# A streaming layer on one core: early weights and stores on GpSimd's queue, and a head's rows fetched by halves

## The chip, the cores and the metric

The kernel runs on one core of a Trainium2 chip. Its time is the device time of one execution in microseconds (us); the figure that counts is the median of several timed runs. Five engines work side by side, each through its own instruction queue in order: PE (matmuls), DVE and ACT (element-wise work), POOL (GpSimd), and SP, which here only issues DMA transfers. GpSimd and ACT can issue transfers too.

## The reference

One inference step of a hybrid layer for 1024 new positions of one stream and 64 of another that has 512 cached keys. All is float32; T = 1088 positions, 1024 channels.

```python
xn = _rmsnorm(x, p['norm_mix_w'])
proj = xn @ p['w_in']
z, xbc, dt_raw, q, k, v, gate_ssm, gate_att = jnp.split(proj, np.cumsum(IN_SIZES)[:-1].tolist(), axis=-1)
xbc_c, conv_new = _causal_dwconv(conv_past, xbc, p['ssm_conv_w'], p['ssm_conv_b'])
...
y_ssm = y_ssm * jax.nn.silu(z)
...
q = _partial_rope(_rmsnorm(q.reshape(b, t, 2 * ATT_HEADS, ATT_HEAD_DIM), p['q_norm_w']), q_pos)
k = _partial_rope(_rmsnorm(k.reshape(b, t, 2 * ATT_HEADS, ATT_HEAD_DIM), p['k_norm_w']), q_pos)
...
o = _diff_attention(q, k_all, v_all, q_pos, k_pos, lam)
o = (_rmsnorm(o, p['subln_w']) * (1.0 - lambda_init)).reshape(b, t, ATT_V_WIDTH)
mix = jax.nn.sigmoid(gate_ssm) * (y_ssm @ p['w_branch_ssm']) + jax.nn.sigmoid(gate_att) * (o @ p['w_branch_attn'])
x = x + mix @ p['w_out']
...
x = x + (jax.nn.silu(hc) * hb) @ p['w_down']
```

In the attention each of 8 heads has two score matrices (two halves, `c` = 0 and 1). Each is softmaxed by itself, and the weights are p0 - lam * p1:

```python
s = jnp.einsum('bqhd,bkhd->bhqk', q, k, preferred_element_type=jnp.float32) * (ATT_HEAD_DIM ** -0.5)
visible = (k_pos[None, :] // CHUNK) <= (q_pos[:, None] // CHUNK)
s = jnp.where(visible[None, None], s, -jnp.inf)
p = jax.nn.softmax(s, axis=-1).reshape(b, ATT_HEADS, 2, nq, -1)
a = p[:, :, 0] - lam * p[:, :, 1]
return jnp.einsum('bhqk,bkhe->bqhe', a.astype(v.dtype), v)
```

## The kernel before

Every float32 operand of a large product is split into a high and a low part, and a product is three matmuls (L156 to L158: high x high, low x high, high x low). The stages follow each other: norm of x with the first values, q, values, k, then attention, the scan of the state-space part, the two branches, the feed-forward part. An instruction scheduler turns the program into one fixed order for each engine; it works from the program's order, priorities (`tc.high_priority`) and pins (`tc.issue_after(x)`: not ahead of x on its queue). What waits for what at run time is then a matter of semaphores: an instruction that waits holds up all that stands behind it on its engine.

The stage of the keys (`heads(B_K, ...)`) ends by writing each of 8 blocks of keys three times: as output (`out_dram<-qr`, L509) and as high and low part into the scratch tensor `k_st` (L480; ACT makes `qh`, DVE makes `ql`, two buffers each). A head reads 64 channels out of all 8 blocks, so its rows can be loaded only when all 16 stores into `k_st` have landed. The queries lie in `q_st` in the same form, the cached keys in `c_st`.

For a head, `head_tiles(h)` loads by SP's queue: `q_t`, `kh_t` and `kl_t` (queries, high and low keys) for both halves, values `v_t`, and the cached `ch_t`, `cl_t`, `cv_t`. A full tile of q, kh or kl is 544 KB, in one or two transfers. `q_t`, `kh_t` and `kl_t` have 3 buffers each, so beside a head's two halves one half of the next fits. `attend(h, i, ...)` works on one block of 128 queries: scores `sc` of both halves (L707, L708), maximum, exponential, difference, then transposes `pt` (L736) and the product with the values `po` (L755). `ATT_ORDER` has the blocks in the order 7, 0, 6, 1, 5, 2, 8, 4, 3.

Attention alone leaves PE with gaps. A generator `stream()` fills them: it yields units of projection (one unit is 24 matmuls into one bank `mm`, over 384 or 320 positions), first gate tiles 15 and 14, then z tiles 0 to 3, then convolution tiles and so on (`ORDER`). `fill(1.9)` after each block takes on average 1.9 units. Each tile (three units) needs one weight block: `raw_weights` loads it (`w_f`, L142), ACT makes `w_hi` (L149), DVE `w_lo` (L150). A gate unit is evacuated by ACT into `gt` and stored into `g_sc` (L594); a z unit by ACT into `zr` (L602) and DVE (L603), and stored into `z_sc` (L604). `gt` and `zr` share three staging buffers. The scheduler lays the first 18 units (six of gates, twelve of z) ahead of head 0's first score.

All of these loads and stores go through `load`, which is SP's queue.

Of the kernel before, what the change touches and what calls it, by code (L numbers as in the profile page):

```python
# [17 lines left out]
P = 128  # L18
D = 1024
KT = D // P  # L20
TP, TS = 1024, 64
# [33 lines left out]
LAST = 200  # L55
ATT_STEPS = 1.9
SCAN_STEPS = 1.5
BRANCH_AT = 4
# [17 lines left out]
def hybrid_layer(ctx: ExitStack, tc: tile.TileContext, xT, xN, prm, cst, rope, wvd, win, wbs, wba, wout, wup, wdn,  # L76
# [53 lines left out]
    extra, turn, ahead, quick, asked, decayed, lowered = None, 0, AHEAD_IN, QUICK, None, None, None  # L130
    emptied = None, None

    def raw_weights(block, k, m, pool=None):
        nonlocal turn
        if pool is None:
            turn = (turn + 1) % 3
        p, b = (pool, 1) if pool is not None else (extra, 1) if extra is not None and turn == 0 else (wp, 2)
        w = p.tile([P, WMAX], F32, name="w_f", tag="w_f", bufs=b)
        hi = p.tile([P, WMAX], R32, name="w_hi", tag="w_hi", bufs=b)
        lo = p.tile([P, WMAX], R32, name="w_lo", tag="w_lo", bufs=b)  # L140
        w, hi, lo = (t[:, : k * m].rearrange("p (k m) -> p k m", k=k) for t in (w, hi, lo))
        load(out=w, in_=block.rearrange("p (k m) -> p k m", k=k))  # L142
        return w, hi, lo
# [8 lines left out]

    def product(ps, terms):
        n = len(terms)
        for i, (a_hi, a_lo, b_hi, b_lo) in enumerate(terms):
            PE.matmul(ps, a_hi, b_hi, start=i == 0, stop=False)  # L156
            PE.matmul(ps, a_hi, b_lo, start=False, stop=False)  # L157
            PE.matmul(ps, a_lo, b_hi, start=False, stop=i == n - 1)  # L158

# [428 lines left out]
    def gate_tiles(tiles):  # L588
        for j in tiles:
            def evac(ps, c, w):  # L590
                nonlocal last_gate
                gt = staged("gt")[:, :w]
                last_gate = act(gt, ps, AF.Tanh, scale=0.5)
                load(out=g_sc[P * j : P * (j + 1), c : c + w], in_=gt)  # L594

            yield from project(win[B_G + j], evac)

    def z_tiles(tiles):
        for j in tiles:
            def evac(ps, c, w):  # L600
                zr = staged("zr")[:, :w]
                act(zr, ps, AF.Tanh, scale=0.5)  # L602
                V.scalar_tensor_tensor(zr, zr, 1.0, ps, ALU.add, ALU.mult)  # L603
                load(out=z_sc[P * j : P * (j + 1), c : c + w], in_=zr)  # L604

# [35 lines left out]
    def stream():  # L641
        for kind, which in ORDER:
            yield from {"c": conv_tiles, "z": z_tiles, "g": gate_tiles}[kind](which)
# [15 lines left out]
    with (tc.tile_pool(name="ak", bufs=1) as ak, tc.tile_pool(name="at", bufs=1) as at,  # L659
          tc.tile_pool(name="psc", bufs=1, space=PSUM) as psc, tc.tile_pool(name="psa", bufs=1, space=PSUM) as pa):  # L660
        def head_tiles(h):
            def fetch(name, n, b, parts):
                t = ak.tile([P, n], R32, name=name, tag=name, bufs=b)
# [12 lines left out]
            ch_t = [fetch("ch_t", PAST, 2, [(0, ck[c][0:64]), (64, ck[c][0:64])]) for c in range(2)]  # L676
            cl_t = [fetch("cl_t", PAST, 2, [(0, ck[c][64:128]), (64, ck[c][64:128])]) for c in range(2)]
            cv_t = ak.tile([P, 4, P], F32, name="cv_t", tag="cv_t", bufs=1)
            load(out=cv_t, in_=cv[:, P * h : P * (h + 1)].rearrange("(a p) e -> p a e", p=P))
            return q_t, kh_t, kl_t, ch_t, cl_t, v_t, cv_t  # L680

        def attend(h, i, tiles, o_t, ssq, s0):
# [7 lines left out]
            for c in range(2):  # L690
# [6 lines left out]
                sc.append(ps)  # L697
                for a in range(0, nk, 512):
                    b = min(512, nk - a)
                    if i < 8:  # L700
                        r_hi, r_lo = kh_t[c][:, a : a + b], kl_t[c][:, a : a + b]
                    elif a == 0:
                        r_hi, r_lo = ch_t[c], cl_t[c]
                    else:
                        r_hi, r_lo = kh_t[c][:, TP:T], kl_t[c][:, TP:T]
                    lhs = q_t[c][:, P * i : P * i + n]
                    PE.matmul(ps[:n, a : a + b], lhs, r_hi, start=True, stop=False)  # L707
                    PE.matmul(ps[:n, a : a + b], lhs, r_lo, start=False, stop=True)  # L708
                if both is None:
# [74 lines left out]

        tiles = head_tiles(0)
        lam = at.tile([P, 4], F32, name="lam")
# [808 lines left out]
```

## Time and profile before

| | |
|---|---|
| three timed runs | 2453.03, 2453.19, 2457.49 us; median 2453.19 |
| the profiled execution | 2448.89 us, span 2447.1 us, mean granted clock 0.999 |
| PE, weight loads, DVE, ACT, POOL busy | 99%, 96%, 65%, 47%, 27% |
| SP's DMA queue (q1) | 385.06 MB, 49.6% of 16 engines |
| GpSimd's DMA queue (q0) | 8.91 MB, 2.4% |
| key stores into `k_st` issued | 337.6 to 378.9 us |
| attention and what fills it | from about 400 to about 1110 us |

The span runs from the first to the last instruction; the execution's own time is 1.8 us longer. Times in the views are us from the span's start. The view of waits lists who waited for whom, with total, count and longest wait; the timeline has start, duration, engine, source line, output and inputs, and in brackets the idle time before. A matmul's duration overlaps its neighbours, so matmuls are best compared from start to start. `SPq` is SP's queue: start of an issue and how long it took; when the data has landed is another matter.

### The profile page before, as it was taken

The numbers are of one execution on the slowest core, as the hardware profiler recorded it, in microseconds if no ns is written. First come the engines' busy times: TensorE is split into PE (matmuls) and PEld (weight loads), VectorE is DVE, ScalarE is ACT, GpSimd is POOL, SyncE is SP. The second block draws the span as 40 slices with busy tenths as digits, with TensorE's granted clock in tenths as the row PEclk, the third lists the DMA queues.
The fourth block names the chain that finished last, engine by engine and source line by source line (L and its number), as shares of the span: only waits on it lengthen the run. The fifth ranks groups of instructions, "written<-read, shape, count | busy, mean of one in ns | idle before, by whom it ended". The sixth has DMA issues, their size and how long they took to land. (4 is left out here: it accounts for less than half of the span.)

```text
span 2447.1 us, 44586 instructions
## 1 busy us (share of the span) xinstructions
PE 2423.5 (99%) x16956; PEld 2350.1 (96%) x16956; DVE 1602.0 (65%) x2755; ACT 1139.8 (47%) x2497; POOL 664.8 (27%) x696
## 2 busy tenths in 40 slices
PE   9999999999999999999999999999999999999998
PEld 8999999999999999999899989999999999999998
DVE  7426254865777667646767785656777777787766
ACT  6334243644565555437664653224543334353532
POOL 0000000100011001004333333103367666755434
PEclk9999999999999999999999999999999999999999
DMA  4218158554453453345679765656234343467874
GB/s 172 84 57 288 64 207 265 142 158 126 131 162 110 130 169 104 98 157 186 217 255 323 223 199 186 193 176 189 63 125 140 117 153 116 147 202 207 218 181 159
DMA packets 269319, 403.55 MB, mean 165 GB/s; under 512 B 33296, under 2 KB 202000, under 8 KB 268976
## 3 DMA queue, kind: packets, MB, share of 16 engines
q1 hardware_dynamic: 258432, 385.06, 49.6%
q0 software_dynamic: 4608, 8.91, 2.4%
q10 hardware_dynamic: 6064, 6.72, 0.8%
q8 instruction: 133, 2.18, 0.4%
q14 instruction: 82, 0.67, 0.1%
HBM read 267.04 MB, written 133.56 MB: 164 GB/s over the span
## 5 line engine op out<-in xcount | busy, mean ns | idle before, releaser
L156 PE MATMUL mm<-xn_hi,w_hi 128*128 128x384 f32 (+1 forms) x1416 | 469.9, 332 | 0.9 <-DVE zr L603 0.9
L158 PE MATMUL mm<-xn_hi,w_lo 128*128 128x384 f32 (+1 forms) x1416 | 468.6, 331 | 0.5 <-DVE w_lo L150 0.5
L157 PE MATMUL mm<-xn_lo,w_hi 128*128 128x384 f32 (+1 forms) x1416 | 467.7, 330 | 0.0
L156 PEld LDWEIGHTS mm<-xn_hi,w_hi 128*128 128x128 f32 x1416 | 266.7, 188 | 4.8 <-issue 1.6
L158 PEld LDWEIGHTS mm<-xn_hi,w_lo 128*128 128x128 f32 x1416 | 266.5, 188 | 3.4 <-issue 1.5
L157 PEld LDWEIGHTS mm<-xn_lo,w_hi 128*128 128x128 f32 x1416 | 266.7, 188 | 2.3 <-issue 1.1
L150 DVE TENSOR_TENSOR w_lo<-w_f,w_hi 128x1024 fp32r<-128x1024 f32 x116 | 147.1, 1270 | 117.9 <-ACT w_hi L149 117.5
L1254 PE MATMUL mx<-n,wh 128*128 128x272 f32 x1076 | 206.0, 289 | 0.7 <-ACT u L1398 0.4
L1254 PE MATMUL mx<-m,w_hi 128*128 128x272 f32 x1010 | 192.9, 289 | 4.2 <-DVE down L1412 4.2
L149 ACT CAST w_hi<-w_f 128x1024 fp32r<-128x1024 f32 x116 | 121.4, 1048 | 145.2 <-PE mm L157 87.5
L1254 PEld LDWEIGHTS mx<-n,wh 128*128 128x128 f32 x1076 | 169.2, 189 | 1.1 <-ACT u L1398 0.6
L1254 PEld LDWEIGHTS mx<-m,w_hi 128*128 128x128 f32 x1010 | 159.3, 189 | 4.6 <-issue 2.8
L1254 PE MATMUL mx<-n,wl 128*128 128x272 f32 x538 | 155.6, 289 | 0.0
L156 PE MATMUL mm<-b_hi,w_hi 128*128 128x384 f32 (+1 forms) x448 | 145.8, 327 | 0.6 <-DVE b_g L224 0.6
L1254 PE MATMUL mx<-m,w_lo 128*128 128x272 f32 x505 | 145.9, 289 | 0.0
L158 PE MATMUL mm<-b_hi,w_lo 128*128 128x384 f32 (+1 forms) x448 | 144.8, 324 | 0.6 <-DVE w_lo L150 0.6
L157 PE MATMUL mm<-b_lo,w_hi 128*128 128x384 f32 (+1 forms) x448 | 145.1, 325 | 0.0
L721 ACT ACTIVATE p_t<-sc,mx 128x1024 f32<-128x1024 f32 (+5 forms) x144 | 106.2, 739 | 76.4 <-DVE mx L712 37.5
L632 DVE SCALAR_TENSOR_TENSOR cc<-pre,par,cc 128x384 f32<-128x384 f32 (+1 forms) x216 | 126.6, 586 | 20.1 <-ACT cc L630 14.9
L620 POOL COPY pre<-pre 128x3 f32<-128x3 f32 x48 | 13.6, 282 | 454.5 <-ACT pre L621 343.6
L1039 ACT CAST w_hi<-ws 128x512 fp32r<-128x512 f32 (+1 forms) x62 | 37.6, 607 | 150.0 <-PE mx L1254 99.2
L618 POOL MEMSET pre<- 128x3 f32 x24 | 2.4, 101 | 383.9 <-PE mx L158 308.5
(418 smaller groups left out, 6735.7 us busy)
## 6 DMA issues: line engine op xcount, KB each, us to landing
w_f<-in_win_dram SPq DMA_DIRECT2D x76, 512.0 KB, 4.1
w_f<-in_wup_dram SPq DMA_DIRECT2D x44, 512.0 KB, 3.8
hr<-q_sc SPq DMA_DIRECT2D x70, 272.0 KB, 4.8
bc<-a_sc SPq DMA_DIRECT2D x32, 512.0 KB, 5.9
q_sc<-hb SPq DMA_DIRECT2D x44, 272.0 KB, 2.3
gb<-q_sc SPq DMA_DIRECT2D x44, 272.0 KB, 3.8
x_sc<-cc SPq DMA_DIRECT2D x48, 192.0 KB, 2.5
q_sc<-gb SPq DMA_DIRECT2D x33, 272.0 KB, 2.3
```

Of the source, the lines that this page charges most:

```text
L149: S.copy(hi, w)
L150: lowered = V.tensor_tensor(out=lo, in0=w, in1=hi, op=ALU.subtract)
L156: PE.matmul(ps, a_hi, b_hi, start=i == 0, stop=False)
L157: PE.matmul(ps, a_hi, b_lo, start=False, stop=False)
L158: PE.matmul(ps, a_lo, b_hi, start=False, stop=i == n - 1)
L618: G.memset(pre[:, 0:3], 0.0)
L620: G.tensor_copy(pre[:, 0:3], tail)
L632: V.scalar_tensor_tensor(cc[:, :m], pre[:, i : i + m], cw(i), cc[:, :m], ALU.mult, ALU.add)
L721: act(p_t[:n, :nk], sc[c][:n, :nk], AF.Exp, bias=mx[:n, c : c + 1], accum_out=dst)
L1039: S.copy(hi, src)
L1254: PE.matmul(ps, w[x][:, c], b[y][:, k], start=start and k == t == 0, stop=k == nk - 1 and t == 2, skip_group_check=not start)
```

## The change

Three things are changed.

1. Nine weight loads (`early_w` counts down from 10) and the stores of the first two entries of `ORDER` (gates 15 and 14, z 0 to 3: 18 stores) are issued by GpSimd instead of SP.
2. `head_tiles` is a generator in three steps: q, kh, kl of half 0; then of half 1 with the values; then the cached rows. Head 0's first two steps are asked for with a high priority. For the later heads the first step is asked for in the head before, at the sixth block (`ASK = 5`), the others at the head's start.
3. In a head's first block (7), a filling unit is taken between the two halves' scores, and half 1's scores are pinned behind its last matmul. That unit comes off the budget of `fill`.

```diff
+ASK = 5
...
     def raw_weights(block, k, m, pool=None):
-        nonlocal turn
+        nonlocal turn, early_w
+        early_w -= 1
...
-        load(out=w, in_=block.rearrange("p (k m) -> p k m", k=k))
+        (G.dma_start if early_w > 0 else load)(out=w, in_=block.rearrange("p (k m) -> p k m", k=k))
...
     def product(ps, terms):
+        nonlocal produced
...
-            PE.matmul(ps, a_lo, b_hi, start=False, stop=i == n - 1)
+            produced = PE.matmul(ps, a_lo, b_hi, start=False, stop=i == n - 1)
...
-                load(out=g_sc[P * j : P * (j + 1), c : c + w], in_=gt)
+                (G.dma_start if early else load)(out=g_sc[P * j : P * (j + 1), c : c + w], in_=gt)
...
-                load(out=z_sc[P * j : P * (j + 1), c : c + w], in_=zr)
+                (G.dma_start if early else load)(out=z_sc[P * j : P * (j + 1), c : c + w], in_=zr)
...
     def stream():
-        for kind, which in ORDER:
+        nonlocal early, early_w
+        early_w = 10
+        for n, (kind, which) in enumerate(ORDER):
+            early = n < 2
             yield from {"c": conv_tiles, "z": z_tiles, "g": gate_tiles}[kind](which)
...
-            q_t = [fetch("q_t", T, 3, [(0, q[0])]), fetch("q_t", T, 3, [(0, q[1][64:128]), (64, q[1][0:64])])]
-            kh_t = [fetch("kh_t", T, 3, [(0, k[c][0:64]), (64, k[c][0:64])]) for c in range(2)]
-            kl_t = [fetch("kl_t", T, 3, [(0, k[c][64:128]), (64, k[c][64:128])]) for c in range(2)]
+            halves = slice(0, 64), slice(64, 128)
+            q_t, kh_t, kl_t = [], [], []
+            for c in range(2):
+                q_t.append(fetch("q_t", T, 3, ([(0, q[0])], [(0, q[1][64:128]), (64, q[1][0:64])])[c]))
+                for t, name, rows in zip((kh_t, kl_t), ("kh_t", "kl_t"), halves):
+                    t.append(fetch(name, T, 3, [(0, k[c][rows]), (64, k[c][rows])]))
+                if c == 0:
+                    yield
...
+        def between():
+            nonlocal spare
+            spare -= 1
+            next(filler)
+            return produced.ins
...
+                pin = tc.issue_after(between()) if c and i == ATT_ORDER[0] else ExitStack()
+                with pin:
+                    for a in range(0, nk, 512):
...
-        tiles = head_tiles(0)
+        asking = head_tiles(0)
+        with tc.high_priority(LAST):
+            next(asking)
+            next(asking)
+        tiles = next(asking)
...
             if h:
-                tiles = head_tiles(h)
+                next(asking)
+                tiles = next(asking)
...
                 next(unit)
+                if x == ASK and h + 1 < 8:
+                    asking = head_tiles(h + 1)
+                    next(asking)
```

How the change moves instructions, at three places. Line numbers of the changed kernel are its own: L480 became L483, L603 L606, L665 L672, L707 and L708 L728 and L729, L150 L152, L156 to L158 L159 to L161.

On SP's queue, the end of the key stores and head 0's loads, before:

```order
L480 DMA k_st<-ql 128x1088
L604 DMA z_sc<-zr 128x384
L480 DMA k_st<-ql 128x1088
L604 DMA z_sc<-zr 128x384
L142 DMA w_f<-in_win_dram 128x1024
L604 DMA z_sc<-zr 128x320
L665 DMA q_t<-q_st 128x1088
L665 DMA q_t<-q_st 64x1088 x2
L665 DMA kh_t<-k_st 64x1088 x4
L665 DMA kl_t<-k_st 64x1088 x4
```

The same place on SP's queue in the changed kernel (`q_t`, `kh_t`, `kl_t` are head 0's, the full 128-row query tile being half 0's):

```order
L483 DMA k_st<-qh 128x1088
L483 DMA k_st<-ql 128x1088 x2
L672 DMA q_t<-q_st 128x1088
L672 DMA kh_t<-k_st 64x1088 x2
L672 DMA kl_t<-k_st 64x1088 x2
L672 DMA q_t<-q_st 64x1088 x2
L672 DMA kh_t<-k_st 64x1088 x2
L672 DMA kl_t<-k_st 64x1088 x2
```

The z stores and the weight load are gone from between the last key stores and the loads, and half 0's three tiles come ahead of half 1's. In the changed kernel the first `q_t` waits for all eight completion semaphores of SP's queue, that is for all transfers before it.

On PE, head 0's first scores, before (`sc_3411` is half 0 of block 7, `sc_3418` half 1; `mm` are filling units):

```order
L157 MATMUL mm_4450<-xn_lo0_88,w_hi_4445 128x384
L158 MATMUL mm_4450<-xn_hi0_87,w_lo_4446 128x384
L707 MATMUL sc_3418<-kh_t_3365,q_t_3359 128x512
L708 MATMUL sc_3411<-kl_t_3368,q_t_3357 128x512
L707 MATMUL sc_3411<-kh_t_3362,q_t_3357 128x512
L708 MATMUL sc_3411<-kl_t_3368,q_t_3357 128x512
L156 MATMUL mm_4486<-xn_hi1_89,w_hi_4445 128x384
```

PE in the changed kernel at the same place:

```order
L160 MATMUL mm_4450<-xn_lo0_88,w_hi_4445 128x384
L729 MATMUL sc_3411<-kl_t_3362,q_t_3357 128x512
L728 MATMUL sc_3411<-kh_t_3359,q_t_3357 128x512
L729 MATMUL sc_3411<-kl_t_3362,q_t_3357 128x512
L161 MATMUL mm_4450<-xn_hi0_87,w_lo_4446 128x384
L159 MATMUL mm_4486<-xn_hi1_89,w_hi_4445 128x384
```

Half 1's first product stood ahead of half 0's second; now half 0's are together, and half 1's first stands 16 filling matmuls after them. The very first score (`sc_3411<-kh_t`) stands 7 rows ahead of the piece shown of before, and now 13 filling matmuls ahead of the `kl_t` row; counted from the start of the program it comes 6 filling matmuls earlier than it did.

On DVE, the evacuation of the second z unit (`zr`), beside the last part of the keys' rotation (`qr`, `t`) and their low parts (`ql`), before:

```order
L524 TENSOR_TENSOR qr<-qr,rp 128x544
L527 TENSOR_TENSOR qr<-qr,t_3317 128x544
L478 TENSOR_TENSOR ql<-qr,qh 128x1088
L603 SCALAR_TENSOR_TENSOR zr<-zr,mm 128x384
L525 TENSOR_TENSOR qr<-qr,t_3316 128x544
L150 TENSOR_TENSOR w_lo<-w_f,w_hi 128x1024
```

DVE in the changed kernel at the same place:

```order
L527 TENSOR_TENSOR qr<-qr,rp 128x544
L606 SCALAR_TENSOR_TENSOR zr<-zr,mm 128x384
L530 TENSOR_TENSOR qr<-qr,t_3317 128x544
L481 TENSOR_TENSOR ql<-qr,qh 128x1088
L528 TENSOR_TENSOR qr<-qr,t_3316 128x544
L152 TENSOR_TENSOR w_lo<-w_f,w_hi 128x1024
```

The evacuation now stands two instructions earlier. Elsewhere in the attention the orders differ by a few matmuls here and there: ahead of head 2's second half on SP's queue a weight load now stands before the keys, ahead of head 3's a gate store and a weight load went behind them. On PE, half 1's last keys are asked for 0.8 us of filling work later than before at head 2, and 1.1 at head 3. From the scan on, all orders are the same, and the number of matmuls is the same in all.

More of the change, by code (lines that the diff above doesn't have):

```diff
@@ L130, in hybrid_layer @@
     extra, turn, ahead, quick, asked, decayed, lowered = None, 0, AHEAD_IN, QUICK, None, None, None
-    emptied = None, None
+    emptied, produced, early, early_w = (None, None), None, False, 0
     def raw_weights(block, k, m, pool=None):
-        nonlocal turn
+        nonlocal turn, early_w
+        early_w -= 1
         if pool is None:
@@ L675, in head_tiles @@
             load(out=v_t[:TS, 8], in_=v[TP:T, P * h : P * (h + 1)])
-            ch_t = [fetch("ch_t", PAST, 2, [(0, ck[c][0:64]), (64, ck[c][0:64])]) for c in range(2)]
-            cl_t = [fetch("cl_t", PAST, 2, [(0, ck[c][64:128]), (64, ck[c][64:128])]) for c in range(2)]
+            yield
+            ch_t, cl_t = ([fetch(name, PAST, 2, [(0, ck[c][rows]), (64, ck[c][rows])]) for c in range(2)]
+                          for name, rows in zip(("ch_t", "cl_t"), halves))
             cv_t = ak.tile([P, 4, P], F32, name="cv_t", tag="cv_t", bufs=1)
             load(out=cv_t, in_=cv[:, P * h : P * (h + 1)].rearrange("(a p) e -> p a e", p=P))
-            return q_t, kh_t, kl_t, ch_t, cl_t, v_t, cv_t
+            yield q_t, kh_t, kl_t, ch_t, cl_t, v_t, cv_t
+        def between():
[3 more added lines that the diff above has]
+            return produced.ins
         def attend(h, i, tiles, o_t, ssq, s0):
@@ L697, in attend @@
                 sc.append(ps)
[L698 to L708, printed above, removed]
+                pin = tc.issue_after(between()) if c and i == ATT_ORDER[0] else ExitStack()
+                with pin:
+                    for a in range(0, nk, 512):
+                        b = min(512, nk - a)
+                        if i < 8:
+                            r_hi, r_lo = kh_t[c][:, a : a + b], kl_t[c][:, a : a + b]
+                        elif a == 0:
+                            r_hi, r_lo = ch_t[c], cl_t[c]
+                        else:
+                            r_hi, r_lo = kh_t[c][:, TP:T], kl_t[c][:, TP:T]
+                        lhs = q_t[c][:, P * i : P * i + n]
+                        PE.matmul(ps[:n, a : a + b], lhs, r_hi, start=True, stop=False)
+                        PE.matmul(ps[:n, a : a + b], lhs, r_lo, start=False, stop=True)
                 if both is None:
```

## The prediction

> **What bounds the kernel now.** I read the page first, then PE's chain of waits, then PE's timeline at the longest waits, then the windows, the SP queue and the DVE around them. The page says that the matmul engine has hardly anything to give.
>
> ```profile
> PE 2423.5 (99%) x16956; PEld 2350.1 (96%) x16956; DVE 1602.0 (65%) x2755; ACT 1139.8 (47%) x2497; POOL 664.8 (27%) x696
> ```
>
> PE is idle 2447.1 - 2423.5 = 23.6 us in the whole span. The change touches only the 700 us of attention and the 75 us ahead of it, so I need PE's waits there.
>
> ```profile
> PE sc L708 <- DMA kl_t<-k_st: 3.3, 3, 2.0
> PE sc L707 <- DMA kh_t<-k_st: 1.3, 1, 1.3
> PE mm L156 <- DVE zr L603: 0.9, 1, 0.9
> ```
>
> In this list of waits (total us, times, longest), the scores `sc` wait four times for a head's keys. PE's timeline shows where (start, duration, group, idle time before it):
>
> ```profile
> 398.56 0.34 PE L156 MATMUL mm<-xn_hi,w_hi 128*128 128x384 f32 x1
> 400.18 0.47 PE L707 MATMUL sc<-kh_t,q_t 128*128 128x512 f32 x1 [1.29 <-DMA kh_t<-k_st]
> ...
> 401.70 0.34 PE L158 MATMUL mm<-xn_hi,w_lo 128*128 128x384 f32 x1
> 402.52 0.47 PE L707 MATMUL sc<-kh_t,q_t 128*128 128x512 f32 x1 [0.47 <-issue]
> 405.01 0.47 PE L708 MATMUL sc<-kl_t,q_t 128*128 128x512 f32 x1 [2.03 <-DMA kl_t<-k_st]
> 405.32 0.42 PE L707 MATMUL sc<-kh_t,q_t 128*128 128x512 f32 x1
> 405.55 0.61 PE L708 MATMUL sc<-kl_t,q_t 128*128 128x512 f32 x1
> 405.96 0.53 PE L156 MATMUL mm<-xn_hi,w_hi 128*128 128x384 f32 x1
> ...
> 408.84 0.41 PE L156 MATMUL mm<-xn_hi,w_hi 128*128 128x384 f32 x1
> 409.08 0.33 PE L157 MATMUL mm<-xn_lo,w_hi 128*128 128x384 f32 x1
> 409.26 0.33 PE L158 MATMUL mm<-xn_hi,w_lo 128*128 128x384 f32 x1
> ```
>
> Matmuls overlap, so I count from start to start. A filling matmul of 384 columns normally starts 0.17 to 0.18 us after the last (409.08 to 409.26), a score of 512 columns 0.23 (405.32 to 405.55). Head 0's scores therefore lose 400.18 - 398.56 - 0.17 = 1.45, 402.52 - 401.70 - 0.17 = 0.65 and 405.01 - 402.52 - 0.23 = 2.26: 4.36 us. Then ten matmuls from 405.55 to 408.84 crawl at 0.32 us apiece. The windows tell why: PEclk, the granted clock, is down.
>
> ```profile
> 340.00:345.00 5.00, 5.00 (x32) 5.00 (x32) 5.00 (x5) 0.68 (x2) 0.00 (x0) 1.00 1.03 403
> 375.00:380.00 5.00, 5.00 (x30) 5.00 (x30) 2.93 (x3) 0.49 (x1) 0.00 (x0) 1.00 1.00 321
> 405.00:410.00 5.00, 4.99 (x19) 4.82 (x20) 3.10 (x5) 1.67 (x3) 0.00 (x0) 0.66 0.71 184
> ```
>
> (Columns: stretch, length, busy time of PE, PEld, DVE, ACT, POOL, clock, DMA share, GB/s.) From 405.55 to 409.08 is 3.53 us where 0.23 + 10 x 0.17 = 1.93 would do: another 1.6 us. Head 0's start costs 4.36 + 1.6 = 5.96, say 6.0 us.
>
> **The change part by part.** *Head 0's loads.* SP's queue shows why the keys were late.
>
> ```profile
> 378.90 0.32 SPq L480 DMA_DIRECT2D k_st<-ql  x1
> 386.46 0.33 SPq L142 DMA_DIRECT2D w_f<-in_win_dram  x1
> 386.88 0.38 SPq L604 DMA_DIRECT2D z_sc<-zr  x1
> 387.44 1.51 SPq L665 DMA_DIRECT2D q_t<-q_st  x3
> 388.99 3.06 SPq L665 DMA_DIRECT2D kh_t<-k_st  x4
> 392.42 5.71 SPq L665 DMA_DIRECT2D kl_t<-k_st  x4
> DMA to landing us min/median/max: 5.4/5.9/6.3
> ```
>
> The last store of the keys leaves at 378.90 and lands 5.4 us later at the soonest (the last line is the answer for the stores `k_st` of the last 5 us), so 384.3. The loads could start then, but a weight load that waits for its buffer and a z store stand ahead of them (386.46, 386.88): they start at 387.44. The change puts both on GpSimd's queue. In the new order the first query load follows the last key store directly and waits until every store of the queue has landed, so it starts at S = 384.3, 3.1 us sooner. It cannot be much sooner: the DMA engines were full from 340 to 380 (shares 1.03 and 1.00), the same bytes still go through them, and DVE makes the last `ql` where it did, because it stands behind a z evacuation there.
>
> ```profile
> 377.12 0.56 DVE L603 SCALAR_TENSOR_TENSOR zr<-zr,mm 128x384 f32<-128x384 f32 x1 [0.95 <-ACT zr L602]
> 377.59 1.29 DVE L478 TENSOR_TENSOR ql<-qr,qh 128x1088 fp32r<-128x1088 f32 x1
> ```
>
> The order of the loads changes too. Before: q of both halves, kh of both, kl of both. The first kh was the third full tile and was there 400.18 - 387.44 = 12.7 us after the start; the first kl, the fifth, at 405.01, 17.6 us after it: 2.4 us a tile. Now the first half's q, kh, kl come first. By that rate they are complete at S + 10.3 = 394.6 (kh, second tile) and 397.0 (kl), and the second half at S + 17.6 = 401.9 (kh) and 404.3 (kl).
>
> When does PE ask? Without any wait PE would have come to its first score at 398.73. It now stands six filling matmuls earlier (1.0 us), and a wait of 0.9 us ahead of it goes (below): 396.8. The first kl follows after 13 matmuls at 399.3, the second half after 16 more and three scores at 402.7, its kl some 2 us later at 404.8. Margins: 2.2, 2.3, 0.8 and 0.5 us. So PE should wait for nothing, with little to spare in the second half. I take the 6.0 us as gained and keep 0.8 us back for the second half.
>
> [...]
>
> *The evacuation of z.* One more wait stands ahead of head 0, two at later heads.
>
> ```profile
> 360.27 0.44 PE L156 MATMUL mm<-xn_hi,w_hi 128*128 128x384 f32 x1 [0.89 <-DVE zr L603]
> 359.67 0.55 DVE L603 SCALAR_TENSOR_TENSOR zr<-zr,mm 128x384 f32<-128x384 f32 x1
> 540.85 0.47 PE L708 MATMUL sc<-kl_t,q_t 128*128 128x512 f32 x1 [0.71 <-DMA kl_t<-k_st]
> 615.73 0.47 PE L708 MATMUL sc<-kl_t,q_t 128*128 128x512 f32 x1 [0.57 <-DMA kl_t<-k_st]
> 358.00 0.49 ACT L602 ACTIVATE zr<-mm 128x384 f32<-128x384 f32 x1
> 358.47 1.28 DVE L478 TENSOR_TENSOR ql<-qr,qh 128x1088 fp32r<-128x1088 f32 x1
> ```
>
> PE waited at 360.27 for a bank that DVE emptied from 359.67 on, behind a `ql` of 1.28. The new order has this evacuation ahead of that `ql`. Its input is ready on ACT at 358.00 + 0.49 = 358.5, so it starts about 1.2 us sooner and the 0.89 us go.
>
> *Heads 2 and 3.* A head's second half goes into the buffer that the head before it frees last, so it is always late. At 615.73 the order has a g store and a weight load moved out from ahead of the keys, and PE comes later by about 1 us of filling work: the 0.57 us go. At 540.85 PE comes about 0.8 us later, but a weight load now stands ahead of the keys; I let its 0.71 stand. Heads 4 to 7 show no wait, so the pinned unit there hides nothing and costs nothing: the filling unit is taken out of the same budget, and the count of matmuls is the same.
>
> *GpSimd's work.* It issues 9 loads and 18 stores more. Its own DMAs near the end of the kernel give the price (L1419; duration, then landing), and its queue is empty there:
>
> ```profile
> L1419 POOL DMA_DIRECT2D out_dram<-down x32: 858/865/1184, 2214.5 to 2379.4; - x32
> DMA to landing us min/median/max: 3.8/5.6/8.4
> 402.62 0.19 POOL L620 COPY pre<-pre 128x3 f32<-128x3 f32 x1 [93.57 <-ACT pre L621]
> ```
>
> 27 x 0.87 = 23.5 us of issuing fit into 93.57 idle us. It comes off no path while a store lands in time (rival B).
>
> Sum: 6.0 + 0.9 + 0.6 - 0.8 = 6.7 us. The profiled execution took 2448.89 us (span 2447.1), so it would take 2442.2. The median of the timed runs is 4.3 us above it, 2453.19; nothing in the profile explains that, and I take the difference off the median: **2446.5 us**. Without the 0.8 kept back it is 2445.7; with the 0.71 too, 2445.0.
>
> **The rivals.** *A: the keys come no sooner (same).* For it: the DMA share of 1.03, and the loads now wait for all stores at once, while GpSimd's transfers take turns with them. If S stays at 387.4, the arrivals are 397.7, 400.1, 405.0 and 407.4 against 396.8, 399.3, 402.7 and 404.8, each later request moved by the waits before it: waits of 0.9, 0, 1.4 and 0.3, together 2.6; none is as long as the 2.03 us ahead of the slow clock. The gain is 6.7 + 0.8 - 2.6 = 4.9, a time of 2448.3. With S 2 us later still, 2 us more are lost and the slow clock's 1.6 come back: 2451.9. Against it: the two instructions that held SP up to 387.44 are gone. I put it at 2450.
>
> *D: new waits in the attention (same).* All orders of the seven heads are shuffled by a few matmuls. If each of the seven later heads waited 0.71 us as head 2 does, 0.71 x 7 - 0.71 = 4.3 us go back: 2450.8. Against it: in 700 us the old order had two such waits.
>
> *B: GpSimd's stores hold up the evacuations (slower).* A z tile is staged in one of three buffers, and ACT fills one every 4.16 us:
>
> ```profile
> 376.59 0.49 ACT L602 ACTIVATE zr<-mm 128x384 f32<-128x384 f32 x1 [2.95 <-PE mm L158]
> 380.75 0.49 ACT L602 ACTIVATE zr<-mm 128x384 f32<-128x384 f32 x1 [3.67 <-PE mm L158]
> DMA to landing us min/median/max: 3.0/6.0/7.3
> ```
>
> So a store has 3 x 4.16 - 1 = 11.5 us from evacuation to landing (the last line: SP's z stores, 7.3 at most). On GpSimd it is 1.18 + 8.4 = 9.6 at the worst row, in a queue where a load can stand ahead with another 1.18. Past 11.5 each excess microsecond stops ACT, then a bank, then PE: 1 us over on the 12 z stores is 12 us, 2446.5 + 12 = 2458.5. For it: the engines are full at 340 to 380. Against it: on a queue of its own a store has fewer ahead. [...]
>
> **How the numbers follow.** Forecast 0.64, A 0.14, D 0.10, B 0.12. What a measurement can tell from no change is about 0.2%, 4.9 us. The forecast is beyond it: faster 0.64. A and D are within it: same 0.24. B: slower 0.12. The forecast's own range is 2444 (a wait or two more gone) to 2448.3. The range takes in A and D up to 2452.5 and, below, 4 us for a timing nearer to the profiled run's: 2441.5 to 2452.5. That leaves out B.
>
> **What would show it.** Right: no wait of `sc` over 0.5 us around 400; clock 1.00 at 405 to 410; the first query load at 383 to 385 directly behind the last key store; no wait at 360 for `zr`; none at head 3 and one below 1.2 us at head 2; a median 5 to 9 us lower. Wrong: the query load at 387 or later (A); ACT or DVE waiting for `z_sc<-zr` or `g_sc<-gt` landings with PE idle behind them (B); several new `sc` waits after 420 (D). The sum fails if the part from 320 to 410 is not shorter by about 6 us.

## The result, and the profile after

Over 22 timed runs each, the changed kernel takes 2447.57 us and the kernel before 2454.44 us (medians). One run of each stood far off (3621.30 and 3955.75 us) and is left out of the ratio. The ratio is 0.9975, with a 95% interval of 0.9969 to 0.9982: 6.1 us less by the ratio, while the two medians are 6.9 apart. The forecast was 2446.5, 6.7 us less.

Head 0 went as forecast. SP's timeline (start, duration, issue) and PE's timeline around the first scores of the changed kernel:

```profile
378.06 0.32 SPq L483 DMA_DIRECT2D k_st<-ql  x1
383.65 0.32 SPq L672 DMA_DIRECT2D q_t<-q_st  x1
```

```profile
396.25 0.39 PE L728 MATMUL sc<-kh_t,q_t 128*128 128x512 f32 x1
...
398.74 0.39 PE L729 MATMUL sc<-kl_t,q_t 128*128 128x512 f32 x1
...
402.20 0.39 PE L728 MATMUL sc<-kh_t,q_t 128*128 128x512 f32 x1
...
404.29 0.39 PE L729 MATMUL sc<-kl_t,q_t 128*128 128x512 f32 x1
```

No row carries a wait in brackets any more. The first query load follows the last key store directly, 3.8 us sooner than before, and the clock stays full behind it. The windows of the changed kernel and then of the kernel before (columns as in the prediction):

```profile
320.00:410.00 90.00, 89.52 (x533) 87.64 (x533) 55.14 (x81) 39.82 (x64) 13.49 (x27) 1.00 0.82 285
...
405.00:410.00 5.00, 5.00 (x35) 5.00 (x34) 4.69 (x10) 3.48 (x9) 0.00 (x0) 1.00 0.76 218
```

```profile
320.00:410.00 90.00, 84.83 (x489) 81.94 (x488) 49.68 (x70) 35.36 (x54) 0.19 (x1) 0.98 0.79 267
```

PE is busy 4.7 us more in this stretch and gets 44 matmuls further. The part that was not forecast stands at head 2. PE's chain of waits between 390 and 1080, where the kernel before had waited three times for `kl_t`:

```profile
PE sc L729 <- DMA kl_t<-k_st: 1.3, 1, 1.3
PE sc L728 <- DMA kh_t<-k_st: 1.1, 1, 1.1
```

Both are at head 2. PE's timeline there, and the granted clock in three stretches of 3.41 us around it (the last section shows why these):

```profile
532.22 0.47 PE L728 MATMUL sc<-kh_t,q_t 128*128 128x512 f32 x1 [1.08 <-DMA kh_t<-k_st]
...
534.88 0.60 PE L729 MATMUL sc<-kl_t,q_t 128*128 128x512 f32 x1 [1.33 <-DMA kl_t<-k_st]
```

```profile
528.24:531.65 3.41, 2.90 (x21) 2.64 (x19) 1.47 (x5) 1.75 (x5) 0.00 (x0) 1.00 1.02 222
531.65:535.07 3.42, 1.52 (x7) 1.22 (x8) 0.00 (x0) 0.00 (x0) 0.00 (x0) 1.00 1.07 237
535.07:538.48 3.41, 3.41 (x12) 3.12 (x12) 1.34 (x2) 0.49 (x1) 0.00 (x0) 0.50 1.02 258
```

From start to start the waits cost 1.24 + 1.49 = 2.73 us (0.87 before), and the stretch at half clock behind them 1.7. At the start of head 1 the changed kernel is 7.25 us ahead of the kernel before (450.39 against 457.64; 6.9 was forecast up to here), at the end of attention only 5.2. The profiled execution itself took 2450.37 us, 1.5 us more than that of before: it has half clock at four places besides the end (12.83, 535.07, 2224.66, 2391.92), the other at two (405.56, 2392.12), and a wait of 2.24 us at 1106.88, for a z unit's evacuation. That one is of the kind that rival B describes, on SP's queue: ACT's evacuation (1105.74) stood 3.62 us for the landing of a z store that SP had issued at 1098.80, behind loads for the scan, and that landed 6.8 us later. The kernel before has no wait of PE there, so part of the lead is spent on it. The last section has what the runs show of how the places at half clock come and go between runs of one program.

### The profile page after: what moved, and what is told of

Read it like the earlier page. It is cut to its first block, busy times and chain, and to the rows that moved or that the text cites. A ratio compares the mean times of both kernels' runs of the same rounds, so it can differ in the third digit from the quotient of the medians.

```text
span 2448.6 us, 44619 instructions
## 1 busy us (share of the span) xinstructions
PE 2424.2 (99%) x16956; PEld 2351.5 (96%) x16956; DVE 1603.0 (65%) x2755; ACT 1141.4 (47%) x2497; POOL 678.4 (28%) x723
## 4 chain that ended last, share of the span: by engine, by line
PE 90%; DVE 3%; DMA 3%; ACT 2%; issue 1%; POOL 0%; SPq 0%; ACTq 0%; DVEq 0%; POOLq 0%
PE mx L1283 17%; PE mm L159 13%; PE mm L161 13%; PE mm L160 12%; PE mm L1283 7%; PE mx L159 5%; PE mx L161 5%; PE mx L160 5%; PE po L776 3%; PE sc L729 2%; DMA hr<-q_sc 2%; PE sc L728 2%; PE pt L757 1%; PE mx L1343 1%; PE yi L902 1%
## 5 line engine op out<-in xcount | busy, mean ns | idle before, releaser
L159 PE MATMUL mm<-xn_hi,w_hi 128*128 128x384 f32 (+1 forms) x1416 | 471.0, 333 | 0.0
L161 PE MATMUL mm<-xn_hi,w_lo 128*128 128x384 f32 (+1 forms) x1416 | 468.3, 331 | 0.4 <-DVE w_lo L152 0.4
L159 PEld LDWEIGHTS mm<-xn_hi,w_hi 128*128 128x128 f32 x1416 | 266.7, 188 | 4.0 <-issue 1.6
L161 PEld LDWEIGHTS mm<-xn_hi,w_lo 128*128 128x128 f32 x1416 | 266.5, 188 | 3.7 <-issue 1.5
L152 DVE TENSOR_TENSOR w_lo<-w_f,w_hi 128x1024 fp32r<-128x1024 f32 x116 | 147.0, 1269 | 110.0 <-ACT w_hi L151 109.4
L159 PE MATMUL mm<-b_hi,w_hi 128*128 128x384 f32 (+1 forms) x448 | 145.9, 327 | 0.6 <-DVE b_g L227 0.6
L161 PE MATMUL mm<-b_hi,w_lo 128*128 128x384 f32 (+1 forms) x448 | 144.8, 324 | 0.6 <-DVE w_lo L152 0.6
L159 PE MATMUL mx<-xn_hi,w_hi 128*128 128x384 f32 (+1 forms) x312 | 104.8, 336 | 2.2 <-DVE zr L606 2.2
```

The source lines that it names most:

```text
L152: lowered = V.tensor_tensor(out=lo, in0=w, in1=hi, op=ALU.subtract)
L161: produced = PE.matmul(ps, a_lo, b_hi, start=False, stop=i == n - 1)
```

## The experiments

My theory: the gain comes from SP being free at the last key store, and part of it is given back at head 2, where a weight load stands ahead of the keys. Rivals: the order by halves alone brings the gain, or the pinned unit; the issuing queue makes no difference, since the bytes are the same. All ratios are to the kernel before, run beside on the same chip.

### Each part alone

Only the queues: `early` and `early_w` put into the kernel before, with its head loads and scores as they were.

> The kernel before with only the queues changed: the first nine filling weights and the stores of g and z ahead of attention are issued by GpSimd; head loads, their order and the scores are those of before (no unit pinned between the halves). Queue theory (what counts is that SP is free at the last key store): first query load at 383 to 385 instead of 387.44, the keys 12.7 us (kh) and 17.6 us (kl) behind it at 396.7 and 401.6, PE asking at about 399 and 402: no wait above 0.5 us, clock 1.00 at 405 to 410, no wait for zr at 360; median 2447 to 2449 against 2454.4 before, nearly the whole gain. Order theory (what counts is that a head's first half is loaded whole before the second): the waits for kh and kl of 1.45 and 2.26 us stay or shrink by less than half; median 2452 to 2454.

Measured: 2450.01 us, ratio 0.999 (0.9981 to 0.9999). The first query load went at 383.58, no score of head 0 waited, the wait for `zr` was gone, the clock was full at 405 to 410: as the queue theory said. But less than half the gain arrived (2.5 of 6.1 us by the ratio). ACT's and PE's timelines show where some of it went:

```profile
420.23 0.71 ACT L631 ACTIVATE cc<-pre,par 128x384 f32<-128x384 f32 x1 [5.76 <-DMA x_sc<-cc]
```

```profile
421.46 3.42 PE L759 MATMUL po<-v_t,a_t 128*128 128x128 f32 x16 [2.03 <-ACT a_t L745]
```

ACT waits 5.76 us for a store of a convolution tile that SP had queued at 412.61 behind all of head 0's loads; PE waits for the copy behind it, and runs at half clock from 421.89. The changed kernel has the same blocked ACT instruction (2.19 us at 420.24), but its copies for PE stand ahead of it.

Only the order: the changed kernel without `early` and `early_w`.

> The changed kernel with all weights and stores back on SP's queue: the loads by halves, the asking in the middle of the head before and the pinned unit stay. Queue theory: a weight load and a z store stand ahead of the first query load again, it starts at about 387.4; kh, kl of the first half at 397.7 and 400.1, of the second at 405.0 and 407.4, while PE asks for the first at about 395: waits of 2 to 3 us and about 2 us at head 0, the clock falls to half once; median 2452 to 2455, no gain. Order theory: the smaller first portion (10.3 us instead of 12.7 to the first keys) covers it: no wait over 0.5 us, median 2447 to 2449.

Measured: 2453.35 us, ratio 1.000 (0.9991 to 1.0009). SP's and PE's timelines:

```profile
386.26 0.33 SPq L144 DMA_DIRECT2D w_f<-in_win_dram  x1
386.68 0.38 SPq L607 DMA_DIRECT2D z_sc<-zr  x1
387.23 0.32 SPq L669 DMA_DIRECT2D q_t<-q_st  x1
```

```profile
397.63 0.47 PE L725 MATMUL sc<-kh_t,q_t 128*128 128x512 f32 x1 [1.74 <-DMA kh_t<-k_st]
...
404.49 0.47 PE L725 MATMUL sc<-kh_t,q_t 128*128 128x512 f32 x1 [1.51 <-DMA kh_t<-k_st]
```

The same two instructions hold SP again and both halves wait, 1.74 and 1.51 us; I had expected 2 to 3 and about 2, and a stretch at half clock, which did not come. Neither part alone brings the gain: the queues bring the keys in time but leave the order that stumbles at 421, the order alone asks too late.

### Which of the two transfers holds SP

The first kernel keeps `early = n < 2` out, the second `early_w = 10`.

> The changed kernel with only the nine weights on GpSimd's queue, the g and z stores on SP's again. My theory (either of the two that stood ahead holds SP): a z store that waits for its evacuation stands between the last key store and the first query load, which goes at 386.5 to 387.3 instead of 383.65; PE asks at about 396.5: waits of 1 to 2 us for the first kh, about 1.5 us at the second half; median 2450 to 2453. Rival (the weight that waits for its buffer is what holds SP): first query load at 383 to 384.5, no waits, median 2446.5 to 2448.5.

> The changed kernel with only the 18 g and z stores on GpSimd's queue, the nine weights on SP's again. My theory: the weight load that waits for its buffer stands ahead of the first query load, which goes at about 386.8; PE asks earlier here (ten filling matmuls fewer ahead, about 395): waits of 2 to 3 us for the first keys; median 2450 to 2454. Rival (the z store is what holds SP): first query load at 383 to 384.5, waits below 0.5 us, median 2446.5 to 2448.5.

Measured: weights alone 2448.75 us, 0.9984 (0.9975 to 0.9993); stores alone 2448.22 us, 0.9982 (0.9972 to 0.9991). SP with only the weights moved, and with only the stores moved:

```profile
386.13 0.32 SPq L607 DMA_DIRECT2D z_sc<-zr  x1
386.63 0.32 SPq L671 DMA_DIRECT2D q_t<-q_st  x1
```

```profile
386.32 0.33 SPq L144 DMA_DIRECT2D w_f<-in_win_dram  x1
386.89 0.32 SPq L671 DMA_DIRECT2D q_t<-q_st  x1
```

Either one holds SP until after 386, as I had said. The times were better than I had expected, since the waits behind it were short: 0.40, 0.82 and 1.03 us at head 0 in the one, 1.11 in the other, and no half clock at head 0. In the profiled executions, taken where both programs have streamed equally many matmul columns, the lead over the kernel before at its start of head 1 (457.64) is 2.4 us with the order alone, 3.7 with the weights moved too, 4.4 with the stores and 7.5 with both. In each, 1.6 us of it is the half clock of the kernel before, which none of the four has there. So most of the lead needs both to be gone. Each of these edits also shifts some matmuls in PE's order, which is not separated here.

### The blocked convolution store

The queues alone, and the stores of the first convolution group on GpSimd too:

```diff
-                load(out=x_sc[P * f : P * (f + 1), c : c + n], in_=cc[:, :n])
+                out = G.dma_start if early_x else load
+                out(out=x_sc[P * f : P * (f + 1), c : c + n], in_=cc[:, :n])
```

> The kernel with only the queues changed, and the stores of the first group of convolution tiles (x_sc<-cc) on GpSimd's queue too. In the run with only the queues, head 0's scores waited for nothing, but ACT stood 5.76 us (up to 420.23) for an x_sc store to land that SP had queued behind all of head 0's loads (issued 412.61, landed 420.13), so that its copy a_t came late and PE waited 2.03 us at 421.46, with the clock at half from 421.89 on. Theory (that blocked store ate 2.2 + 1.7 = 3.9 us of the gain): ACT's wait below 1 us, PE's wait at 421 below 0.5 us, no half clock there; median 3 to 4 us lower than with only the queues (2450.0): 2446 to 2447. Rival (a head's loads by halves are what counts, the wait at 421 is made good later): median 2449 to 2451.

Measured: 2449.63 us, 0.9988 (0.9979 to 0.9997). ACT's wait and PE's wait at 421 are gone, with the half clock behind them. In the profiled execution the lead at the start of head 1 follows: 7.6 us instead of 3.4. The timed runs follow less clearly: the medians are 0.4 us apart, the means 1.9 (2451.06 and 2449.12, eleven runs each), with a scatter of about 1 us in that difference. The orders behind head 0 changed too, and PE waits 0.65 and 0.92 us at head 2 and 0.81 at 1081 for the scan's first input. That the store caused the wait is shown; what it is worth in the timed runs is not, nor why they stay above the changed kernel's.

### The pinned unit

```diff
-                pin = tc.issue_after(between()) if c and i == ATT_ORDER[0] else ExitStack()
+                pin = ExitStack()
```

> The changed kernel without the pinned unit: no filling unit is drawn and queued between the two halves' scores of a head's first tile. At head 0 the order of the matmuls is the same with and without it. My theory: the pin hides nothing in heads 3 to 7, median 2446 to 2449 as the changed kernel (2447.6), head 2's two waits stay near 1.2 and 1.5 us. Rival (the pin is what covers the late second halves): waits of 0.5 to 1.5 us for kh_t or kl_t at three or more of the later heads, median 2450 to 2454.

Measured: 2446.82 us, 0.9971 (0.9961 to 0.9982), with head 2's waits at 0.70 and 1.27 us. No gain of the pin can be told from these seven runs.

### Head 2: the weight ahead of the keys

The 17th filling weight, which SP loads ahead of head 2's keys, goes to GpSimd.

```diff
-        (G.dma_start if early_w > 0 else load)(...)
+        (G.dma_start if early_w > 0 or early_w == -7 else load)(...)
```

> The changed kernel with one more weight load on GpSimd's queue: the 17th of the filling weights, which in the changed kernel stands on SP directly ahead of the keys of head 2's second half (issued at 521.54, landed at 525.85; the keys behind it landed at 531.88 and 534.75, with PE waiting 1.08 and 1.33 us, and the clock at half from 535.07 to 538.48). Theory (the load ahead in the same queue holds the keys up by 1.2 us or more): both waits below 0.3 us and no half clock there, median 4 us lower than the changed kernel, 2443 to 2444.5. Rival (the same bytes go through the same 16 DMA engines, whoever issues them): keys land as late, waits of 1 us and more stay, median 2446.5 to 2449.

```profile
532.61 0.47 PE L728 MATMUL sc<-kh_t,q_t 128*128 128x512 f32 x1 [1.31 <-issue]
...
535.11 0.47 PE L729 MATMUL sc<-kl_t,q_t 128*128 128x512 f32 x1 [0.49 <-DMA kl_t<-k_st]
```

(`issue`: the profile names nothing that was waited for; the keys for this score landed 0.2 us before it.) Measured: 2449.13 us, 0.9979 (0.9970 to 0.9988). My theory fell. The keys landed at 532.41 and 534.97, no sooner than from behind the weight (531.88 and 534.75); the second wait is shorter only because four more matmuls of filling stand ahead of it. The rearranged filling also made a new wait of 1.43 us at 610.51. The shares of the DMA engines ahead of attention agree with these landings: from 340 to 380 us SP's transfers take 74.3% of the 16 DMA engines' time and GpSimd's 26.5% in the changed kernel, SP's alone 101.6% in the kernel before, at 383 and 384 GB/s. At head 0 it was the order on SP's queue that counted: with two instructions on it that were not ready, SP came to the first query load at 387.44, without them at 383.65.

So the bytes themselves: the same weight, one eighth of it loaded and the rest zeros. This kernel leaves out part of a product; it serves for the times alone.

```diff
+        if early_w == -7: G.memset(w[:, 1:], 0.0); block, k = block[:, :m], 1
...
+        (G.dma_start if early_w > 0 else load)(out=w[:, :k], in_=block.rearrange("p (k m) -> p k m", k=k))
```

> The changed kernel, with the 17th filling weight (on SP's queue, directly ahead of the keys of head 2's second half) loading one eighth of its block; the rest is filled with zeros by GpSimd, so this tile's products are left out of the result. Byte theory (the six transfers of the second half and this weight share the DMA engines, and 0.46 MB fewer at some 220 GB/s are 2.1 us): the second half's kh lands at about 529.8 and kl at 532.6 instead of 531.88 and 534.75; with PE asking for kh at 531.0 and, since no filling matmul stands between here, for kl at 531.2, waits of 0 and 1.4 us instead of 1.08 and 1.33 plus the fill, no half clock; median 2 to 3.5 us below the changed kernel, 2444 to 2445.5. Place theory (a load ahead in the queue costs a fixed latency, whatever its size): landings as before within 0.5 us, waits of 1.0 and 2.5 us and half clock; median 2447 to 2449.

```profile
533.41 0.47 PE L730 MATMUL sc<-kl_t,q_t 128*128 128x512 f32 x1 [1.78 <-DMA kl_t<-k_st]
```

Measured: 2446.58 us, 0.9979 (0.9971 to 0.9988), not to be told from the changed kernel. The keys landed at 530.92 and 533.27, 1.0 and 1.5 us sooner instead of 2.1. The weight's bytes are thus the smaller part. The six transfers of the second half take 11 us by themselves (issued from 522.22, the last landed at 533.27). With three buffers they cannot be issued sooner: their buffers are those of head 1's first half, whose last scores began at 521.79 and 522.03. PE needs the keys 9 us later.

### More filling between the halves

In PE's order the filling runs ahead of the program at head 2: drawing two to six units there instead of one leaves the order as it is. Eight at head 2 and three at head 3 do move it.

```diff
-                pin = tc.issue_after(between()) if c and i == ATT_ORDER[0] else ExitStack()
+                pin = tc.issue_after(between({2: 8, 3: 3}.get(h, 1))) if c and i == ATT_ORDER[0] else ExitStack()
```

> The changed kernel with more filling units drawn and queued between the halves' scores at two heads: eight at head 2 and three at head 3 instead of one. The filling runs so far ahead of the program that up to six units change nothing at head 2; with eight, 9.3 us instead of 4.3 us of matmuls stand between the start of the head and its second half's first score, at head 3 some 7.7. Theory (head 2's keys are late because their buffer comes free only 9 us ahead of their use, while weight and keys need 12.5 us; any 4 us more of filling hide that): head 2's keys asked at about 536, after their landing at 532 to 535; no wait of sc over 0.3 us there and no half clock; median 3 to 4.4 us below the changed kernel run beside it: 2443 to 2444.5. Rival (the filling taken ahead is missing later): new waits of 1 us and more behind head 3, median as the changed kernel or above, 2446.5 to 2450.

```profile
537.25 0.39 PE L729 MATMUL sc<-kh_t,q_t 128*128 128x512 f32 x1
537.48 0.39 PE L730 MATMUL sc<-kl_t,q_t 128*128 128x512 f32 x1
```

Measured: **2442.64 us**, 0.9964 (0.9951 to 0.9978), the lowest median of all. The last key landed at 533.80, 3.7 us ahead of its use, and from 390 to 1080 PE has no wait that the chain lists. The changed kernel, run beside it once more, unaltered:

> The changed kernel once more, unaltered, beside the others. Theory (a half-clock stretch follows where PE was idle for more than about 2.0 us of one 3.41 us period of a fixed grid, and where the grid lies against the program differs from run to run): head 0, 360 and the order of all work as in the first profile; the waits at head 2 stay at 0.7 to 1.5 us each, while the half-clock stretches at 12.83, 535.07, 2224.66 and 2391.92 come or go; median 2446 to 2449. Rival (the half clock belongs to the waits alone): the same four stretches at the same places within 1 us.

```profile
532.55 0.47 PE L728 MATMUL sc<-kh_t,q_t 128*128 128x512 f32 x1 [0.61 <-DMA kh_t<-k_st]
534.88 0.47 PE L729 MATMUL sc<-kl_t,q_t 128*128 128x512 f32 x1 [0.99 <-DMA kl_t<-k_st]
```

Measured: 2446.08 us, 0.9976 (0.9966 to 0.9986). The half clock at 535 and at 2392 did not come back, that at 2224 came again (2219.84), and the stretch at the start was twice as long (6.83 us from 11.42). The wait at 1106 shrank from 2.24 to 0.35 (at 1103.53): the z store in question took 5.5 us to land instead of 6.8, and ACT stood 2.63 us for it instead of 3.62. Why it landed sooner, I cannot say. The version with eight and three units is 3.4 us below this one by the medians; the two intervals overlap. At the same clock of 0.999 its four runs average 2443.1 us, the changed kernel's eight (both sets) 2446.1.

### ACT's queue instead of GpSimd's

> The changed kernel with the nine weights and 18 stores issued by ACT instead of GpSimd. Theory (what counts is to be off SP, and that the issuing engine has nothing that is waited for): first query load at 383 to 385 as in the changed kernel, head 0's keys in time; but a weight load that waits for its buffer now stands in ACT's own queue ahead of evacuations, so PE waits for ACT between 320 and 385, some six times 0.3 to 1 us; median 2449 to 2453. Rival (ACT, 47% busy, has room enough): no new PE wait over 0.5 us ahead of attention, median 2446 to 2449.

Measured: 2445.82 us, 0.9972 (0.9961 to 0.9982). My theory fell, the rival holds: the first query load goes at 384.49, and PE's waits between 320 and 385 are one of 0.4 us, which is in the changed kernel too. Three waits for `kl_t` stand further on (0.35, 0.84 and 0.84 us), and PE's order differs from head 0 on, so the two times do not compare the queues alone. What counts at head 0 is to be off SP.

### Waits made on purpose

The version with eight and three units, in which heads 1 to 7 load some rows of `kl_t` again.

```diff
+                    again = {1: 1, 2: 2, 3: 2, 4: 3, 5: 2, 6: 3, 7: 2}.get(h, 0) if c and name == "kl_t" else 0
+                    t.append(fetch(name, T, 3, [(0, k[c][rows]), (64, k[c][rows])] + [(64, k[c][rows])] * again))
```

> The version with eight and three units between the halves, in which heads 1 to 7 load the lower half of their second half's kl_t once to three times more than needed (the same rows to the same place), so that these keys land some 3 to 10 us later: waits of PE are made on purpose at several heads, to see which of them is followed by the half clock. Grid theory: PE's granted clock changes only on a grid of 3.41 us periods, and a period at half clock follows exactly where PE stood idle for more than about 2.0 us of the 3.41 us period before it; a single wait of less than 2.0 us never has one, whatever its place, and every wait of 4.8 us or more (it holds 2.0 us of some period, wherever the grid lies) has one. Rival 1 (the clock falls only after a period that is idle throughout, 3.41 us): none after waits below 3.4 us. Rival 2 (it falls after any wait over about 1 us): a half-clock stretch directly behind each such wait. All half-clock stretches lie a whole number of 3.41 us apart by the grid theory.

Measured: 2473.41 us in one run. Four of PE's seven waits, and the windows around three of them, on the grid of 3.41 us that the last section describes:

```profile
620.91 0.47 PE L731 MATMUL sc<-kl_t,q_t 128*128 128x512 f32 x1 [1.75 <-DMA kl_t<-k_st]
...
714.68 0.50 PE L731 MATMUL sc<-kl_t,q_t 128*128 128x512 f32 x1 [2.06 <-DMA kl_t<-k_st]
...
812.07 0.77 PE L731 MATMUL sc<-kl_t,q_t 128*128 128x512 f32 x1 [2.75 <-DMA kl_t<-k_st]
...
1007.06 0.50 PE L731 MATMUL sc<-kl_t,q_t 128*128 128x512 f32 x1 [2.58 <-DMA kl_t<-k_st]
```

```profile
712.51:715.93 3.42, 1.36 (x10) 1.16 (x10) 1.12 (x2) 1.16 (x3) 0.18 (x1) 1.00 0.90 274
715.93:719.34 3.41, 3.41 (x14) 3.31 (x13) 2.07 (x6) 2.72 (x6) 0.00 (x0) 0.50 0.62 181
808.09:811.50 3.41, 1.23 (x9) 0.96 (x7) 1.84 (x8) 2.04 (x3) 0.17 (x1) 1.00 1.07 258
811.50:814.91 3.41, 2.84 (x9) 2.58 (x10) 2.29 (x9) 0.00 (x0) 0.00 (x0) 0.50 0.42 134
1002.65:1006.07 3.42, 1.83 (x14) 1.48 (x12) 1.20 (x3) 2.64 (x6) 0.00 (x0) 1.00 0.47 117
1006.07:1009.48 3.41, 2.42 (x13) 2.29 (x14) 1.34 (x3) 3.16 (x7) 0.31 (x2) 1.00 0.31 106
```

Waits of 1.29 and 1.75 us had no half clock, 2.06, 2.75, 3.63 and 6.32 had. That of 2.58 had none: a border of the grid cuts it, and PE was busy 1.83 us of the one period and 2.42 of the next. The wait of 2.06 fell into one period whole. Both rivals are out, in this one run.

## Why the prediction came out right

- **Head 0, 6.0 us: right.** The first load went at 383.65 (384.3 forecast). PE came to its four scores at 396.25, 398.74, 402.20 and 404.29 (forecast 396.8, 399.3, 402.7, 404.8). The last transfer of each tile landed at 390.29, 395.16, 399.93 and 402.32, two to four microseconds sooner than by the rate that I took from the kernel before, so the 0.8 us that I kept back was not needed. What stands ahead of head 1 is 7.25 us shorter, where I had named about 6 as the sign of the sum. Rival A is out.
- **The wait for `zr`, 0.9: right.** It is gone; it came back where the stores and weights returned to SP (0.90 us at 360), and where only the weights (0.89) or only the stores (0.43) did.
- **Head 3, 0.6: right,** no wait. **Head 2: the step that failed.** I wrote "I let its 0.71 stand" and "below 1.2 us". It became 1.08 and 1.33 us, 1.9 us more from start to start, and in the first profile a stretch at half clock on top (in the second profile the waits cost 1.0 us more than before, without half clock). I had looked at what stands ahead in SP's queue and not counted what has to pass between the release of a buffer and its next use: a weight and six transfers, 12.5 us from 522.25 to 534.75, in 9 us. This is rival D at one head instead of seven.
- **GpSimd, nothing: right.** POOL is busy 678.4 us instead of 664.8. An issue took 0.54 us there, less than the 0.87 to 1.18 that I had priced; a store landed up to 9.9 us after it, more than the 8.4. Only one store on GpSimd's queue held an evacuation up, by 0.18 us at 395.77, and PE had no wait from it: rival B is out. What did hold ACT up, for 2.2 us at 420 without harm to PE, was a store left on SP.
- **The pinned unit, nothing: right.** I had argued from the budget; without the pin PE's order is the same up to 697, in head 4, so in heads 0 to 3 it did not move anything.
- **The slow clock, 1.6 us: right in the place, wrong as a price.** At head 0 the half clock is gone in both profiles of the changed kernel. But in the runs it went with how idle one period of the grid was (2.71 us in the one ahead of 405.56, from start to start), not with one wait: that of 2.58 us made on purpose had no half clock behind it, that of 2.06 had. Over the runs whose clock is on record (76 of the kernel before, 29 of the changed one) the mean granted clock rose from 0.9979 to 0.9982, an estimated 0.6 us of 2450, not 1.6. Over these same runs the means differ by 5.6 us (2452.8 and 2447.2). At equal clock the changed kernel is 4.9 us faster at 0.997 (2449.0 against 2453.9), 5.4 at 0.998, 5.3 at 0.999 and 5.8 at 1.000, each with a scatter of 0.4 to 0.8. So nearly all of the gain is waits (6.7 - 1.6 = 5.1 forecast).
- **The sum came out partly by luck.** The rows give 4.4 + 0.9 + 0.6 us of waits gone and 1.0 to 1.9 lost at head 2, so 4.0 to 4.9, with 0.6 for the clock 4.6 to 5.5. The smaller clock term and the loss at head 2, both missed, were in part made good by the 0.8 kept back; the rest of the 6.1, some 0.6 to 1.5 us, is within the scatter of the runs and not accounted for.
- **The profiled execution and the median.** I took over a difference of 4.3 us that "nothing in the profile explains". The clock explains part of it: the profiled execution had 0.999, and the runs of the kernel before average 2451.5 us there, 2453.9 at 0.997. It lies 2.6 us below the average of its own clock, and that stays open.

## What to carry to other kernels

With two transfers that were not ready ahead of it on SP's queue, the first query load went at 387.44, without them at 383.65. So look at what stands ahead of the load that is waited for, and move what is not ready there to another engine's queue: ACT's served as well as GpSimd's (384.49 and 383.65). Moving a transfer made no bandwidth here: head 2's keys landed at 532.41 and 534.97 with the weight on GpSimd's queue, at 531.88 and 534.75 with it on SP's. Where a buffer came free too late for the bytes behind it, work put ahead of the use hid the wait, and one must look in the final order whether it got there; one more buffer was not tried.

## What the runs showed of the hardware

In these runs the granted clock stepped on a grid. In each of the ten profiles with more than one stretch at half clock, all of them begin a whole number of 3.413 us apart (in the changed kernel 12.83, 535.07, 2224.66 and 2391.92 are 153, 495 and 49 periods apart); the other four have only one, at the end.

The clock of a period went with how idle PE was in the one before. I summed PE's idle time, from start to start beyond the normal spacing (0.174 us for 384 columns, 0.147 for 320, 0.231 for 512, 0.111 for 128), for each period of the grid between 320 and 1100 (attention) and between 2200 and 2440, in all 14 profiles. All 21 periods at full clock with more than 2.06 us of it were followed by a period at half clock; of those with 1.98 or less none was. Two lay at the border: 2.055 was followed, 2.057 was not. For instance, 2.71 us from 402.15 in the kernel before and 2.13 from 531.65 in the changed one were followed by half clock, 1.79 from 398.73 in the kernel before was not. In these stretches the line thus lay near 60% of a period; spacings taken 4% smaller move it to 2.10 us. In the scan, whose small matmuls have no such clear spacing, the sum is unsafe: it gives up to 2.0 or 2.3 us, depending on the spacing, and no period there was at half clock. At head 0 the half clock cost the kernel before 1.6 us; my estimate for a whole period is up to 1.7, half its length: at 535 PE did 12 matmuls in the period at half clock, and 25 in 3.40 us at full clock in the changed kernel's second run.

The grid lay against the program differently from run to run: counted from the start of the span its borders stand 2.79 us past a whole number of periods in the kernel before, 2.59 in the changed kernel, 1.18 in its second run. PE's longest wait for `down` was 2.6 us in both runs of the changed kernel; the half clock at 2392 came in the first and not in the second. That is part of the scatter: the changed kernel's runs average 2443.7 us at clock 1.000 and 2449.0 at 0.997. A single profile can mislead by as much: the first one of the changed kernel (2450.37 us) shows no gain over that of before (2448.89).
